# Differences of cumulated decays in a Mamba-2 block: rows broadcast from DRAM and GpSimd subtractions in place of float32r products

## The chip, the cores and the metric

The kernel runs on one core of a Trainium2 chip. The metric is the device time of one execution in microseconds (us); the time before is 1030.11 us, the median of 3 runs (1029.46 to 1030.83). The engines are PE (TensorE, matrix products; PEld its weight loads), DVE (VectorE), ACT (ScalarE), POOL (GpSimd) and SP (SyncE, which issues the weight loads). Each engine works through its own queue in order.

## The reference, cut to what matters

One layer: adaLN and RMSNorm on 256 context and 256 latent tokens, one input projection, a bidirectional Mamba-2 scan (32 heads in 8 groups of 4, chunks of 128 tokens) beside a gated MLP group, one output projection. The part that the change touches is the decay matrix of the diagonal blocks, in both directions (the backward one on flipped tokens):

```
a = dtc * A.reshape(G, R)
acs = jnp.cumsum(a, axis=2)
...
diff = acs_t[..., :, None] - acs_t[..., None, :]
mask = jnp.tril(jnp.ones((Q, Q), dtype=bool))
Lmat = jnp.exp(jnp.where(mask, diff, -jnp.inf))
y_diag = jnp.einsum('bcgqk,bcgrqk,bckgrp->bcqgrp', CB, Lmat, xdt)
```

Forward and backward differences have opposite signs on the two sides of the diagonal, so the kernel takes exp of the smaller of the two and applies the triangles to CB.

## The kernel before, in words

All large products run in three float32r passes (weights split into a high part on ACT, line 79, and a low part on DVE, line 80; lines 123 to 125 or 840 to 842 multiply). In this text a *main product* is one of these: 128 columns of weights against 512 columns. Weights come as 1 MB pieces from SP, each good for 48 main products of a full tile.

The program has four parts: the startup (scale and shift columns of adaLN, the token-rate column block `dt`, and seven tiles of the x/B/C columns), the 25 other x/B/C tiles (lines 652 to 669), 64 pieces of weights for the latents' v, u and gate columns (from 474 us on), and the output projection. A group g of the scan owns four tiles: two of x, one of B, one of C.

Between the main products the program places pieces of other work. `later(dt, fn)` notes a piece with a due time, `pump` emits it when the running count of product time reaches it; the order that the engines then get is also arranged by a scheduler, which moves instructions within a queue. `plan_tile` sets the due times of a group: `conv_silu`, `ssd_x` (transposes `ptx` to `xk`), `ssd_w` (POOL scales `xk` to `xw` and `xl`), `ssd_b`, `ssd_e` (the decay matrix `E`), `ssd_cb` (`pcb`, masked on DVE to `cbf` and `cbb`), `ssd_states` (`psc`, `psl`, then `hs` over ACT, POOL and DVE), `ssd_y` for the two chunks c (POOL makes a first part of `M`, DVE adds the other and multiplies by `E`; `pso` from `hs`; three sums into `y` on POOL) and `ssd_yd` (`psy` from `M`). A name such as M(1,0) below is `M` of group 1, chunk 0. Groups 0 to 2 follow each other closely, since most of their tiles are left over from the startup; groups 3 to 7 come every 47.7 us.

The decay matrix before: `dt_rows` (line 483) puts four copies of the step decays (`ar`, on POOL, line 486) against triangles of ones, so that `psa` has the cumulated sums of all 32 heads four times on 128 partitions; ACT and DVE split them into float32r parts and build two operands, `Lb` (minus the sums, and ones) and `Rm` (the sums of each of four heads beside ones, line 498, with a constant half from line 505). `ssd_e` (line 545) masks `Lb` to the heads of the group on ACT (`L`), then makes four products of 128x512 (`pd`, line 553), which give q minus k for four heads; ACT copies the backward one to `E`, DVE takes the minimum with the forward one (line 556), ACT takes exp.

```
q = spt([P, 4, P], f"pd{g}{c}{d}")
nc.tensor.matmul(q, lhsT=L[:, d * 2 + c, :], rhs=Rm[:, d * 2 + c], start=True, stop=True)
...
nc.scalar.copy(E[:, c], pd[1])
nc.vector.tensor_tensor(E[:, c], pd[0], E[:, c], op=ALU.min)
```

The functions that the change touches, with the line numbers of the profile:

Of the kernel before, what the change touches and what calls it, by code (L numbers as in the profile page):

```python
# [39 lines left out]
def tile_hybrid_ssd_mlp(  # L40
# [396 lines left out]
    dl4 = cpool.tile([P, 4], F32, name="dl4")
    gm = cpool.tile([P, NGRP], F32, name="gm")
    nc.vector.tensor_reduce(dl4, ident.rearrange("p (m h) -> p h m", h=4), axis=mybir.AxisListType.X, op=ALU.add)
    nc.vector.tensor_reduce(gm, ident.rearrange("p (b g h) -> p g b h", b=4, g=8), axis=mybir.AxisListType.XY, op=ALU.add)  # L440
# [13 lines left out]
    ar = y[:, 1, 256:512].rearrange("p (d r h) -> p d r h", d=2, r=4)  # L454
# [26 lines left out]
    # rows of acs, split exactly in two float32r parts, for the differences on the tensor engine:  # L481
    # rows (hi, lo) x 32 heads carry acs[q], rows (hi, lo) x 32 heads carry -acs[k]
    def dt_rows():
        psa = spt([P, 4, P], "psa")
        for c in range(2):
            nc.gpsimd.tensor_copy(ar, bc(at[:, 3 * c, :].rearrange("p (d h) -> p d h", d=2), 2, 4))
            for d in range(2):
                nc.tensor.matmul(psa[:, d * 2 + c, :], lhsT=ar[:, d].rearrange("p r h -> p (r h)"),
                                 rhs=tri_le if d == 0 else tri_ge, start=True, stop=True)
        X = yseg(6).bitcast(F32R)  # L490
        XL = yseg(7).bitcast(F32R)
        psf = psa.rearrange("p a b -> p (a b)")
        nc.scalar.copy(X, psf)
        nc.vector.tensor_tensor(XL, psf, yseg(6), op=ALU.subtract)
        for r0 in (32, 96):
            nc.vector.tensor_copy(X[r0 : r0 + 32], yseg(7)[r0 : r0 + 32])
        Xv = yseg(6).rearrange("p (a b) -> p a b", a=4)
        nc.vector.tensor_tensor(Rm[0:64], bc(Xv[0:64], 2, 4),
                                dl4[0:64].unsqueeze(1).unsqueeze(3).to_broadcast([64, 4, 4, P]), op=ALU.mult)
# [45 lines left out]
    def ssd_e(g):  # L545
        L = cv1.tile([P, 4, P], F32R, tag="L", name=f"L{g}")
        nc.scalar.mul(L, Lb, gm[:, g : g + 1])
        E = cv1.tile([P, 2, 4, P], F32, tag="E", name=f"E{g}")
# [473 lines left out]
```

## Time and profile before

| what | value |
|---|---|
| median of 3 runs | 1030.11 us (1029.46 to 1030.83) |
| span of the profiled execution, first to last instruction | 1026.3 us |
| median less span | 3.8 us |
| PE busy | 1000.6 us (97%) |
| DVE, ACT, POOL busy | 624.9, 474.9, 130.0 us |
| mean granted TensorE clock | 0.991 of full speed |

No time of its own is listed for the profiled execution beside its span; the 3.8 us by which the median of the runs exceeds the span are taken for what lies around the span. Busy time of PE is modelled from pipelined products that overlap, so a PE that is 97% busy can still be made faster by taking products away. What one product costs in the queue is read from the distance of the starts of its neighbours.

### The profile page before, as it was taken

Reading aid. Unit: us, or ns where it says so; the run is one execution under the profiler, and the core shown is the slowest. Engines: PE = TensorE matmul, PEld = TensorE weight load, DVE = VectorE, ACT = ScalarE, POOL = GpSimd, SP = SyncE. Lnnn points to the kernel's source line nnn. Section 1 sums busy time; section 2 is a strip of 40 time slices with the busy share of each in tenths; the row PEclk is TensorE's granted clock in tenths of the full one; section 3 lists DMA queues with packets and bytes.
Section 4 is the critical chain, followed back from the end, with each engine's and each line's share of the span. In section 5 each row is a group of like instructions: output and inputs, shape, how many; then the busy total and the mean of one; then the engine's idle time right before and its main releaser. Section 6 shows DMA issues by size and latency. Waiting matters only on the chain. (4 is left out here: it accounts for less than half of the span.)

```text
span 1026.3 us, 12875 instructions
## 1 busy us (share of the span) xinstructions
PE 1000.6 (97%) x5040; PEld 794.0 (77%) x5040; DVE 624.9 (61%) x927; ACT 474.9 (46%) x664; POOL 130.0 (13%) x169
## 2 busy tenths in 40 slices
PE   7999999999999999999999999999999999999995
PEld 2566777777888888787888888887888888888884
DVE  4443459997666565756566867666555564444446
ACT  4333346654534353435555344454565563444333
POOL 1000012272213233233000000000000000000004
PEclk9899999999999999999999999999999999999998
DMA  9999752221322222323878778774555545555542
GB/s 354 417 406 339 278 205 83 83 83 44 121 82 83 83 82 82 123 82 125 291 283 321 283 253 296 272 296 164 169 201 174 195 164 205 202 179 193 193 176 82
DMA packets 30028, 198.74 MB, mean 194 GB/s; under 512 B 3552, under 2 KB 3696, under 8 KB 7312
## 3 DMA queue, kind: packets, MB, share of 16 engines
q1 hardware_dynamic: 28224, 192.44, 50.8%
q0 software_dynamic: 1024, 4.28, 1.5%
q10 hardware_dynamic: 720, 1.20, 0.3%
q8 instruction: 39, 0.64, 0.2%
q14 instruction: 21, 0.17, 0.0%
HBM read 195.81 MB, written 2.10 MB: 193 GB/s over the span
## 5 line engine op out<-in xcount | busy, mean ns | idle before, releaser
L80 DVE TENSOR_TENSOR lo_w<-w,hi_w 128x1024 fp32r<-128x1024 f32 x242 | 298.6, 1240 | 222.4 <-ACT hi_w L79 222.1
L79 ACT CAST hi_w<-w 128x1024 fp32r<-128x1024 f32 x242 | 254.3, 1052 | 337.1 <-PE pa L842 143.8
L840 PE MATMUL pa<-hi_w,hhi 128*128 128x512 f32 x512 | 201.9, 395 | 0.0
L841 PE MATMUL pa<-lo_w,hhi 128*128 128x512 f32 x512 | 199.6, 390 | 0.0
L842 PE MATMUL pa<-hi_w,hlo 128*128 128x512 f32 x512 | 199.4, 389 | 0.0
L123 PE MATMUL psx<-hhi,hi_w 128*128 128x512 f32 (+1 forms) x400 | 152.5, 381 | 0.4 <-DVE acc L424 0.3
L124 PE MATMUL psx<-hlo,hi_w 128*128 128x512 f32 (+1 forms) x400 | 146.7, 367 | 0.0
L125 PE MATMUL psx<-hhi,lo_w 128*128 128x512 f32 (+1 forms) x400 | 146.3, 366 | 0.0
L840 PEld LDWEIGHTS pa<-hi_w,hhi 128*128 128x128 f32 x512 | 96.1, 188 | 20.9 <-issue 1.6
L842 PEld LDWEIGHTS pa<-hi_w,hlo 128*128 128x128 f32 x512 | 96.1, 188 | 20.2
L841 PEld LDWEIGHTS pa<-lo_w,hhi 128*128 128x128 f32 x512 | 96.2, 188 | 19.2 <-issue 0.2
L123 PEld LDWEIGHTS psx<-hhi,hi_w 128*128 128x128 f32 x400 | 75.6, 189 | 14.1 <-issue 2.4
L124 PEld LDWEIGHTS psx<-hlo,hi_w 128*128 128x128 f32 x400 | 75.6, 189 | 13.1 <-issue 2.2
L125 PEld LDWEIGHTS psx<-hhi,lo_w 128*128 128x128 f32 x400 | 75.5, 189 | 12.5 <-issue 0.2
L424 DVE SCALAR_TENSOR_TENSOR acc<-psx,pc,acc 128x248 f32<-128x248 f32 (+1 forms) x204 | 84.1, 469 | 0.8 <-ACT acc L411 0.2
L701 DVE SCALAR_TENSOR_TENSOR junk<-gate,cb 128x2048 bf16<-128x2048 f32 x16 | 36.7, 2292 | 28.4 <-DMA gate<-in_wada_dram 28.4
L912 POOL TENSOR_TENSOR og<-ob,G 128x512 f32<-128x512 f32 x7 | 10.5, 1535 | 333.1 <-DVE ob L907 333.1
L887 PE MATMUL pq<-hi_w,yal 128*128 128x512 f32 x128 | 50.7, 396 | 0.0
L885 PE MATMUL pq<-hi_w,yah 128*128 128x512 f32 x128 | 50.7, 396 | 0.0
L886 PE MATMUL pq<-lo_w,yah 128*128 128x512 f32 x128 | 50.7, 396 | 0.0
L278 DVE SCALAR_TENSOR_TENSOR xT<-xT,ha,y 128x256 f32<-128x256 f32 x32 | 14.1, 482 | 60.1 <-ACT ha L210 60.0
L885 PE MATMUL pm<-hi_w,hhi 128*128 128x512 f32 x128 | 50.0, 390 | 0.0
(221 smaller groups left out, 1305.6 us busy)
## 6 DMA issues: line engine op xcount, KB each, us to landing
w<-in_wlat_dram SPq DMA_DIRECT2D x64, 1024.0 KB, 4.8
ada<-in_wada_dram SPq DMA_DIRECT2D x32, 1024.0 KB, 7.8
w<-in_wout_dram SPq DMA_DIRECT2D x32, 1024.0 KB, 4.8
w<-in_wxbc_dram SPq DMA_DIRECT2D x25, 1024.0 KB, 4.8
gate<-in_wada_dram SPq DMA_DIRECT2D x16, 1024.0 KB, 6.0
wst<-in_wst_dram SPq DMA_DIRECT2D x16, 480.0 KB, 8.4
xT<-in_xch_dram SPq DMA_DIRECT2D x4, 1024.0 KB, 10.1
xf<-in_xtok_dram SPq DMA_DIRECT2D x2, 1024.0 KB, 4.7
```

The lines of the kernel that those rows point to most:

```text
L79: nc.scalar.copy(hi, raw)
L80: nc.vector.tensor_tensor(lo, raw, hi.bitcast(F32), op=ALU.subtract)
L123: nc.tensor.matmul(ps, lhsT=whi, rhs=hhi[k][:, s], start=start, stop=False)
L124: nc.tensor.matmul(ps, lhsT=whi, rhs=hlo[k][:, s], start=False, stop=False)
L125: nc.tensor.matmul(ps, lhsT=wlo, rhs=hhi[k][:, s], start=False, stop=stop)
L424: nc.vector.scalar_tensor_tensor(ao, zi, cw[:, k : k + 1], ao, op0=ALU.mult, op1=ALU.add)
L840: nc.tensor.matmul(pa[tk], lhsT=hhi[k][:, t], rhs=whi[:, w], start=k == 0, stop=False)
L841: nc.tensor.matmul(pa[tk], lhsT=hhi[k][:, t], rhs=wlo[:, w], start=False, stop=False)
L842: nc.tensor.matmul(pa[tk], lhsT=hlo[k][:, t], rhs=whi[:, w], start=False, stop=k == KT - 1)
L885: nc.tensor.matmul(p, lhsT=yh[:, t], rhs=whi[:, w], start=j == 0, stop=False)
L886: nc.tensor.matmul(p, lhsT=yh[:, t], rhs=wlo[:, w], start=False, stop=False)
L887: nc.tensor.matmul(p, lhsT=yl[:, t], rhs=whi[:, w], start=False, stop=j == 15)
```

## The change

`ssd_e` no longer uses PE. `dt_rows` forms the cumulated sums once, 32 heads on 32 partitions (`arow`), and GpSimd's queue writes them to a DRAM tile `acs` (64 KB). For each group `row_load` reads the group's four heads (8 KB) back onto all 128 partitions (`R`, 1 MB in SBUF, one buffer, again from GpSimd's queue). The new `dt_cols` turns `arow` by four small transposes into columns `acol`, k on partitions. In `ssd_e` POOL subtracts the columns from `R` in place (two instructions of 128x1024, one for each chunk) and DVE takes the minimum of the two directions from SBUF. The masked operand, the operands' construction, the copies from `pd` and their PSUM banks go. `row_load(0)` is called behind the write, `row_load(g + 1)` at the end of `ssd_states(g)`; `dt_rows` comes at 5 of the running count and `dt_cols` at 7, where `rm_const` and `dt_rows` stood. The rest of the diff takes comments away.

```diff
+    drp = ctx.enter_context(mkpool(name="drp", bufs=1, space=bass.MemoryType.DRAM))
...
-    Rm = cv1.tile([P, 4, 4, P], F32R, name="Rm")
-    Lb = cv1.tile([P, 4, P], F32, name="Lb")
...
+    acol = cv1.tile([P, 4, 32], F32, name="acol")
+    arow = cv1.tile([32, 4, P], F32, name="arow")
+    acs = drp.tile([32, 4 * P], F32, name="acs")
...
     def dt_rows():
-        psa = spt([P, 4, P], "psa")
-        for c in range(2):
-            nc.gpsimd.tensor_copy(ar, bc(at[:, 3 * c, :].rearrange("p (d h) -> p d h", d=2), 2, 4))
...
+        psa = spt([32, 4, P], "psa")
+        for d in range(2):
+            for c in range(2):
+                nc.tensor.matmul(psa[:, d * 2 + c, :], lhsT=at[:, 3 * c, d * 32 : (d + 1) * 32],
                                  rhs=tri_le if d == 0 else tri_ge, start=True, stop=True)
-        X = yseg(6).bitcast(F32R)
...
-        nc.vector.tensor_scalar(Lb[64:128], Xv[64:128], -1.0, None, op0=ALU.mult)
...
+        nc.scalar.copy(arow, psa)
+        nc.gpsimd.dma_start(acs, arow.rearrange("h a q -> h (a q)"))
+        row_load(0)
+
+    def dt_cols():
+        pst = spt([P, 4, 32], "pst")
+        for a in range(4):
+            nc.tensor.transpose(pst[:, a, :], arow[:, a, :], ident[0:32, 0:32])
+        nc.vector.tensor_copy(acol, pst)
...
+    def row_load(g):
+        R = cv1.tile([P, 4, 2, 2, P], F32, tag="R", name=f"R{g}")
+        nc.gpsimd.dma_start(R.rearrange("p h d c q -> p (h d c q)"),
+                            acs[4 * g : 4 * g + 4, :].rearrange("h x -> (h x)").unsqueeze(0).partition_broadcast(P))
+        rows_[g] = R
...
     def ssd_e(g):
-        L = cv1.tile([P, 4, P], F32R, tag="L", name=f"L{g}")
-        nc.scalar.mul(L, Lb, gm[:, g : g + 1])
+        R = rows_.pop(g)
         E = cv1.tile([P, 2, 4, P], F32, tag="E", name=f"E{g}")
         for c in range(2):
-            pd = []
-            for d in range(2):
-                q = spt([P, 4, P], f"pd{g}{c}{d}")
-                nc.tensor.matmul(q, lhsT=L[:, d * 2 + c, :], rhs=Rm[:, d * 2 + c], start=True, stop=True)
-                pd.append(q)
-            nc.scalar.copy(E[:, c], pd[1])
-            nc.vector.tensor_tensor(E[:, c], pd[0], E[:, c], op=ALU.min)
+            Rc = R[:, :, :, c, :]
+            col = acol.rearrange("p (d c) h -> p c h d", c=2)[:, c, 4 * g : 4 * g + 4, :]
+            nc.gpsimd.tensor_tensor(Rc, Rc, bc(col, 3, P), op=ALU.subtract)
+            nc.vector.tensor_tensor(E[:, c], Rc[:, :, 0, :], Rc[:, :, 1, :], op=ALU.min)
         nc.scalar.activation(E, E, AF.Exp)
...
         S["hs"] = hs
+        if g + 1 < NGRP:
+            row_load(g + 1)
...
-    later(5, rm_const)
+    later(5, dt_rows)
     later(6, dt_decay)
-    later(7, dt_rows)
+    later(7, dt_cols)
```

Where instructions stand in the queues, at three places. On PE, behind the main products of the tile in which the step decays become ready (`psd` are the products for the other decays, `ptx00` the first transposes of group 0), before:

```order
L475 MATMUL psd_1348<-y_127,ones_70 128x64
L488 MATMUL psa_1364<-tri_le_72,y_127 128x128
L488 MATMUL psa_1364<-tri_ge_75,y_127 128x128
L123 MATMUL psx8_1413<-hhi5_97,hi_w2_1290 128x512
L124 MATMUL psx8_1413<-hlo5_113,hi_w2_1290 128x512
L488 MATMUL psa_1364<-tri_le_72,y_127 128x128
L488 MATMUL psa_1364<-tri_ge_75,y_127 128x128
L125 MATMUL psx8_1413<-hhi5_97,lo_w2_1291 128x512
L521 MATMUL ptx00_1449<-ident_65,xbc0_1387 128x128 x4
```

and with the change:

```order
L484 MATMUL psa_1333<-tri_le_72,y_127 32x128 x2
L484 MATMUL psa_1333<-tri_ge_75,y_127 32x128 x2
L472 MATMUL psd_1354<-y_127,tri_lt_78 128x96
...
L472 MATMUL psd_1354<-y_127,ones_70 128x64
L123 MATMUL psx8_1412<-hhi5_97,hi_w2_1292 128x512
L124 MATMUL psx8_1412<-hlo5_113,hi_w2_1292 128x512
L493 MATMUL pst_1370<-ident_65,arow_1299 128x32 x4
L125 MATMUL psx8_1412<-hhi5_97,lo_w2_1293 128x512
L518 MATMUL ptx00_1448<-ident_65,xbc0_1386 128x128 x4
```

The four `psa` products stand together ahead of `psd`, and the new transposes `pst` stand where the second pair of `psa` stood.

On POOL, from the start of group 0 to its second `M`, before:

```order
L486 COPY y_127<-y_127 128x256 x2
L530 TENSOR_TENSOR xw0_1505<-xk0_1448,ed_1295 128x256 x4
L533 TENSOR_TENSOR xl0_1510<-xk0_1448,ed_1295 128x256 x2
L609 TENSOR_TENSOR y_127<-xk0_1448,dsk_84 128x256 x2
L575 TENSOR_TENSOR hs0_1652<-hs0_1652,ed_1295 128x256 x2
L597 TENSOR_TENSOR M00_1671<-cbb0_1637,dtt_1294 128x512
L610 TENSOR_TENSOR y_127<-y_127,yo00_1680 128x256
L597 TENSOR_TENSOR M01_1734<-cbb0_1637,dtt_1294 128x512
```

and with the change:

```order
L487 DMA acs_1300<-arow_1299 32x512
L500 DMA R0_1340<-acs_1300 128x2048
L527 TENSOR_TENSOR xw0_1504<-xk0_1447,ed_1297 128x256 x4
L530 TENSOR_TENSOR xl0_1509<-xk0_1447,ed_1297 128x256 x2
L604 TENSOR_TENSOR y_127<-xk0_1447,dsk_84 128x256
L548 TENSOR_TENSOR R0_1340<-R0_1340,acol_1298 128x8x128 x2
L604 TENSOR_TENSOR y_127<-xk0_1447,dsk_84 128x256
L500 DMA R1_1648<-acs_1300 128x2048
L568 TENSOR_TENSOR hs0_1641<-hs0_1641,ed_1297 128x256 x2
L548 TENSOR_TENSOR R1_1648<-R1_1648,acol_1298 128x8x128 x2
L592 TENSOR_TENSOR M00_1662<-cbb0_1626,dtt_1296 128x512
L592 TENSOR_TENSOR M01_1725<-cbb0_1626,dtt_1296 128x512
```

The subtractions of group 0, the read for group 1 and the subtractions of group 1 all stand ahead of M(0,0).

On POOL again, around the two `M` of group 1, before:

```order
L575 TENSOR_TENSOR hs1_1895<-hs1_1895,ed_1295 128x256 x2
L597 TENSOR_TENSOR M10_1938<-cbb1_1880,dtt_1294 128x512
L610 TENSOR_TENSOR y_127<-y_127,yo10_1947 128x256
L611 TENSOR_TENSOR y_127<-y_127,yo10_1947 128x256
L597 TENSOR_TENSOR M11_2006<-cbb1_1880,dtt_1294 128x512
```

and with the change:

```order
L500 DMA R2_1883<-acs_1300 128x2048
L527 TENSOR_TENSOR xw2_1802<-xk2_1763,ed_1297 128x256 x4
L530 TENSOR_TENSOR xl2_1807<-xk2_1763,ed_1297 128x256 x2
L568 TENSOR_TENSOR hs1_1876<-hs1_1876,ed_1297 128x256 x2
L548 TENSOR_TENSOR R2_1883<-R2_1883,acol_1298 128x8x128
L592 TENSOR_TENSOR M10_1921<-cbb1_1861,dtt_1296 128x512
L548 TENSOR_TENSOR R2_1883<-R2_1883,acol_1298 128x8x128
L605 TENSOR_TENSOR y_127<-y_127,yo10_1930 128x256
L606 TENSOR_TENSOR y_127<-y_127,yo10_1930 128x256
L592 TENSOR_TENSOR M11_1979<-cbb1_1861,dtt_1296 128x512
```

One subtraction for group 2 now precedes M(1,0) and the other stands between M(1,0) and M(1,1); likewise both subtractions for group 3 come between M(2,0) and M(2,1).

## Rows read from the trace of the kernel before

**Rows 1.** First lines of the page: span, then engine, busy us (share), instructions.

```profile
span 1026.3 us, 12875 instructions
PE 1000.6 (97%) x5040; PEld 794.0 (77%) x5040; DVE 624.9 (61%) x927; ACT 474.9 (46%) x664; POOL 130.0 (13%) x169
```

**Rows 2.** Windows: stretch, length, busy us (count) by engine, clock, DMA share, GB/s.

```profile
160.00:205.00 45.00, 43.51 (x213) 34.55 (x212) 42.44 (x93) 30.60 (x43) 11.86 (x17) 1.00 0.20 71
205.00:250.00 45.00, 44.39 (x230) 35.08 (x229) 39.42 (x75) 24.08 (x33) 27.94 (x34) 1.00 0.20 71
250.00:475.00 225.00, 224.95 (x1138) 185.35 (x1137) 141.44 (x257) 99.07 (x132) 58.80 (x73) 1.00 0.25 89
```

**Rows 3.** Waits of PE, 100 to 1000 us: us in total, times, longest.

```profile
PE pso L604 <- DVE hs L576: 1.9, 2, 1.4
PE psa L488 <- POOL y L486: 1.2, 1, 1.2
PE psx L123 <- DVE acc L424: 0.3, 1, 0.3
```

**Rows 4.** Timeline of PE: start us, us, instruction; four transposes, then the four `pd` of group 0.

```profile
180.08 0.60 PE L541 MATMUL ptb<-ident,xbc 128*128 128x128 f32 x4
180.44 1.17 PE L553 MATMUL pd<-Rm,L 128*128 128x512 f32 x4
181.45 0.39 PE L124 MATMUL psx<-hlo,hi_w 128*128 128x512 f32 x1
181.67 0.39 PE L125 MATMUL psx<-hhi,lo_w 128*128 128x512 f32 x1
```

**Rows 5.** Timeline of PE at the cumulated sums.

```profile
165.00 0.40 PE L124 MATMUL psx<-hlo,hi_w 128*128 128x512 f32 x1
166.58 0.49 PE L488 MATMUL psa<-tri_le,y 128*128 128x128 f32 x2 [1.19 <-POOL y L486]
```

**Rows 6.** Single lines of code: duration ns min/median/max, first and last start, forms.

```profile
L530 POOL TENSOR_TENSOR xw<-xk,ed x32: 608/615/662, 172.5 to 455.0; 128x256 f32<-128x256 f32 x32
L597 POOL TENSOR_TENSOR M<-cbb,dtt x16: 1037/1042/1887, 197.5 to 483.7; 128x512 f32<-128x512 f32 x16
L609 POOL TENSOR_TENSOR y<-xk,dsk x16: 610/838/1597, 176.0 to 458.3; 128x256 f32<-128x256 f32 x16
L80 DVE TENSOR_TENSOR lo_w<-w,hi_w x242: 1207/1226/1703, 146.9 to 1004.3; 128x1024 fp32r<-128x1024 f32 x121
```

**Rows 7.** DMA issues: count, KB each, median us from issue to landing.

```profile
cb<-in_crow_dram POOLq DMA_DIRECT2D x1, 1024.0 KB, 4.8
G<-in_gpost_dram POOLq DMA_DIRECT2D x1, 1024.0 KB, 6.8
out_dram<-xf SPq DMA_DIRECT2D x4, 256.0 KB, 2.3
dtc<-in_dtp_dram POOLq DMA_DIRECT2D x1, 32.0 KB, 7.1
```

**Rows 8.** Timeline of POOL: M(0,0), M(1,0), M(2,1), M(7,0).

```profile
197.47 1.04 POOL L597 TENSOR_TENSOR M<-cbb,dtt 128x512 f32<-128x512 f32 x1 [7.66 <-DVE cbb L589]
219.09 1.04 POOL L597 TENSOR_TENSOR M<-cbb,dtt 128x512 f32<-128x512 f32 x1
245.06 1.04 POOL L597 TENSOR_TENSOR M<-cbb,dtt 128x512 f32<-128x512 f32 x1 [2.79 <-PE psy L619]
473.17 1.89 POOL L597 TENSOR_TENSOR M<-cbb,dtt 128x512 f32<-128x512 f32 x1 [14.29 <-DVE cbb L589]
```

**Rows 9.** Timeline of PE: psy(0,0), psy(1,0) and psy(2,1), the products that take M.

```profile
201.87 1.00 PE L619 MATMUL psy<-xk,M 128*128 128x64 f32 x8
226.07 1.00 PE L619 MATMUL psy<-xk,M 128*128 128x64 f32 x8
249.40 1.00 PE L619 MATMUL psy<-xk,M 128*128 128x64 f32 x8
```

**Rows 10.** Timeline of DVE: M(1,0) is multiplied by E.

```profile
222.78 0.68 DVE L602 TENSOR_TENSOR M<-M,E 128x512 f32<-128x512 f32 x1
```

More of the change, by code (lines that the diff above doesn't have):

```diff
@@ L434, in tile_hybrid_ssd_mlp @@
     ed = cv1.tile([P, 384], F32, name="ed")
-    Rm = cv1.tile([P, 4, 4, P], F32R, name="Rm")
-    Lb = cv1.tile([P, 4, P], F32, name="Lb")
[L437 to L440, printed above, removed]
+    acol = cv1.tile([P, 4, 32], F32, name="acol")
+    arow = cv1.tile([32, 4, P], F32, name="arow")
+    acs = drp.tile([32, 4 * P], F32, name="acs")
     eu = ed.rearrange("p (u h) -> p u h", h=32)
@@ L453, in tile_hybrid_ssd_mlp @@
     eat = ed[:, 320:384].rearrange("p (d h) -> p d h", d=2)
-    ar = y[:, 1, 256:512].rearrange("p (d r h) -> p d r h", d=2, r=4)
     def dt_final():
@@ L483, in dt_rows @@
     def dt_rows():
-        psa = spt([P, 4, P], "psa")
-        for c in range(2):
-            nc.gpsimd.tensor_copy(ar, bc(at[:, 3 * c, :].rearrange("p (d h) -> p d h", d=2), 2, 4))
-            for d in range(2):
-                nc.tensor.matmul(psa[:, d * 2 + c, :], lhsT=ar[:, d].rearrange("p r h -> p (r h)"),
-                                 rhs=tri_le if d == 0 else tri_ge, start=True, stop=True)
-        X = yseg(6).bitcast(F32R)
[L491 to L499, printed above, removed]
-        nc.vector.tensor_scalar(Lb[64:128], Xv[64:128], -1.0, None, op0=ALU.mult)
-    nc.gpsimd.memset(Lb[0:64], 1.0)
-    def rm_const():
-        nc.gpsimd.tensor_copy(Rm[64:128], dl4[64:128].unsqueeze(1).unsqueeze(3).to_broadcast([64, 4, 4, P]))
+        psa = spt([32, 4, P], "psa")
+        for d in range(2):
+            for c in range(2):
+                nc.tensor.matmul(psa[:, d * 2 + c, :], lhsT=at[:, 3 * c, d * 32 : (d + 1) * 32],
+                                 rhs=tri_le if d == 0 else tri_ge, start=True, stop=True)
+        nc.scalar.copy(arow, psa)
[6 more added lines that the diff above has]
+        nc.vector.tensor_copy(acol, pst)
+    rows_ = {}
+    def row_load(g):
[3 more added lines that the diff above has]
+        rows_[g] = R
     gs_ = {}
@@ L545, in ssd_e @@
     def ssd_e(g):
-        L = cv1.tile([P, 4, P], F32R, tag="L", name=f"L{g}")
-        nc.scalar.mul(L, Lb, gm[:, g : g + 1])
+        R = rows_.pop(g)
         E = cv1.tile([P, 2, 4, P], F32, tag="E", name=f"E{g}")
         for c in range(2):
-            pd = []
-            for d in range(2):
-                q = spt([P, 4, P], f"pd{g}{c}{d}")
-                nc.tensor.matmul(q, lhsT=L[:, d * 2 + c, :], rhs=Rm[:, d * 2 + c], start=True, stop=True)
-                pd.append(q)
-            nc.scalar.copy(E[:, c], pd[1])
-            nc.vector.tensor_tensor(E[:, c], pd[0], E[:, c], op=ALU.min)
+            Rc = R[:, :, :, c, :]
+            col = acol.rearrange("p (d c) h -> p c h d", c=2)[:, c, 4 * g : 4 * g + 4, :]
+            nc.gpsimd.tensor_tensor(Rc, Rc, bc(col, 3, P), op=ALU.subtract)
+            nc.vector.tensor_tensor(E[:, c], Rc[:, :, 0, :], Rc[:, :, 1, :], op=ALU.min)
         nc.scalar.activation(E, E, AF.Exp)
```

## The prediction, made before the changed kernel was run

> **What bounds the kernel now.** I read the page first: the span is 1026.3 us, and PE is busy for 97% of it [rows 1]. [...] Third, the waits of PE: after the startup only three kinds are left, 3.4 us in all [rows 3]. So PE sets the end nearly everywhere. The exception to look at is 160 to 250 us, where groups 0 to 2 crowd together: DVE is busy for 42.4 of 45 us and then 39.4, and POOL goes from 11.9 to 27.9 us of 45 [rows 2]. The change adds its work to POOL, so this stretch decides what is left of the gain.
>
> **The change part by part.** The timed runs have a median 3.8 us above the profiled span; I take that as fixed and count against 1026.3.
>
> *The products that go.* Four `pd` per group start at 180.44 us and the next main product at 181.45; main products follow each other at 0.22 to 0.23 us [rows 4]. Four at that distance are 0.9 us; 1.01 holds the refill that any such block has. For 8 groups: 7.2 us (bounds 7.0 and 8.1). All of it is on PE's path.
>
> *The cumulated sums.* The second pair of `psa` starts at 166.58 us, behind a main product that began at 165.00; 0.23 us of that is the product, so PE stood for 1.35 us, for POOL's copy `ar` [rows 3, 5]. This copy is gone. In its place PE waits for ACT's `arow` before `pst`. Between the end of `psa` and `pst` lie now six `psd` products and two main products, some 1.7 us, and ACT needs about 0.6 for the copy: no wait expected. Four 128x128 transposes take 0.36 us (180.08 to 180.44) [rows 4]; the smaller `pst` is put at that. Net 1.0 us gained; if `arow` is late, up to 1.35 is lost again.
>
> *Two other waits.* The main product that waited 0.3 us for DVE's convolution [rows 3] had a DVE that was also building `Rm` and `Lb`; four instructions, about 4 us, go there, so 0.3 is gained. `pso` waited 1.9 us in two places for `hs`, the longest 1.4 in group 7 [rows 3]. There M(7,0) started on POOL at 473.17 after waiting for `cbb`, took 1.89 us beside DVE's splits, and `hs` of group 7 queued behind it [rows 8]. With the change the order puts `pcb` of group 7 five main products earlier and `pso` two later, so the chain has 1.6 us more room: 1.4 gained, and 0.5 in group 1 from the smaller `pd` load. Together 2.2 us (bounds 0.5 and 2.2).
>
> So far 7.2 + 1.0 + 2.2 = 10.4 us.
>
> *What POOL, DMA and DVE get instead.* No row shows a 128x1024 subtraction on POOL. Two-input instructions take 0.615 us for 256 elements per partition and 1.04 for 512 [rows 6], a slope that gives 1.9 us for 1024. That is the value without DVE's interference; L609 goes from 0.61 to 1.60 us for the same shape, and DVE's split from 1.21 to 1.70 [rows 6], when both work from SBUF. Bounds: 1.9 and 3.8 (twice). I take 1.9, with 0.5 more per group where the queue orders put DVE's splits and `M` beside it. A 1 MB load over POOL's queue lands after 4.8 or 6.8 us [rows 7]: 5.8. The write of 64 KB is bounded by 2.3 us (a store from SP) and 7.1 (a small load over POOL's queue at the start) [rows 7]; I take 3, since the 7.1 stood beside the startup's loads.
>
> Group 0: `psa` is done at about 164, `arow` at 164.8, the write at 168, R0 lands at 174.3, while POOL is at `xw` until 175.6. Subtractions to 179.5, minimum to 181.1, R1 requested then and landed at 187.4, its subtractions to about 192. M(0,0) started at 197.47 after 7.66 us of waiting for `cbb` [rows 8]: the subtractions of group 1 fit into that hole, and `cbb` comes some 3.3 us earlier since DVE has less to do. PE wants psy(0,0), before at 201.87 [rows 9], six main products sooner in the order (1.4) and 2.2 us sooner for the gains so far: 198.3; M needs 4.2 us on POOL and DVE from 194.2: ready at 198.4. Wait 0.1 to 0.2.
>
> Group 1: psy(0,0) and the transposes behind it let ACT finish `xk` of group 1 at about 202.5. POOL then has ten instructions of 0.61 us (`xw`, `xl`, `y`) and two sums of about 0.75 ahead of the request for R2: 202.5 + 6.1 + 1.5 + 0.5 = 210.6; R2 lands at 216.5. Eight more of 0.61 (`xw` and `xl` of group 2, `hs` of group 1) end at 215.5; the first subtraction waits for R2 and runs to 218.9, then M(1,0), before at 219.09 [rows 8]. It needed 4.4 us until DVE had it multiplied at 223.46 [rows 10]; 0.4 more beside the second subtraction: 223.7. PE, ahead by 1.0 + 0.3 + 0.5 + 3 x 0.9 less the waits so far, 3.7 us, wants psy(1,0), before at 226.07 [rows 9], at 222.4. Wait 1.3.
>
> Group 2: M(1,1) starts at 225.4, behind psy(1,0) and the two sums; DVE needs some 6 us until it has multiplied it and taken the minimum of group 2. R3 is requested at 232, lands at 237.8, two subtractions and the two sums that follow end at 243.6, where M(2,1) starts, before at 245.06 [rows 8]. PE, 2 us ahead, wants psy(2,1), before at 249.40 [rows 9], 4.3 us behind M(2,1) and with no room, at 247.4; it is ready at 243.6 + 4.3 = 247.9. Wait 0.5. Four small waits of 0.3 on the same chains (psy(0,1), `pso` of groups 1 and 2, psy(1,1)): 1.2. Together 3.2 us; bounds 0 and, with every term at its upper bound, about 20 (below).
>
> From group 3 on, groups are 47.7 us apart and the order computes `E` one group ahead: read and subtractions stand at the head of POOL's round. POOL was busy for 58.8 of 225 us [rows 2], 12.5 in 47.7; with 4.3 more and a read of 5.8 it still stands idle for half of the time: hidden. If that cover were gone, `xw` and then `psc` would be late. The minimum is the same work for DVE; ACT loses two copies and the mask per group; the DMA share rises by 1 MB per group from 0.25: hidden.
>
> Sum: 10.4 - 3.2 = 7.2 us; 1030.1 - 7.2 = **1022.9 us**.
>
> [...]
>
> **The rivals.**
>
> *Everything fits* (chance 0.17): the early waits vanish, because reads land in 4.8 us and PE's slack is larger than I read. For it: PE's own waits were tiny. 1030.1 - 10.4 = 1019.7.
>
> *The early groups eat the gain* (0.11): waits of 8.4 to 12.4 us there. It decides if both the subtractions cost 3 us or more and reads land at 6.8. Time 1030.1 to within 0.2%.
>
> *POOL becomes the pace of groups 0 to 2* (0.10), slower. The mechanism: POOL stops at each first subtraction until its read has landed, and `M`, `hs` and `xw` stand behind it. With the write at 7.1, reads at 6.8 and subtractions at 3.8: R0 lands at 179.7, subtracted at 187.3; R1 at 195.9, subtracted at 203.5; psy(0,0) at 207.8, a wait of 9.5. At psy(1,0) the wait is 2.4 + 0.8 longer: 4.5. At psy(2,1) 4.3 longer: 4.8. With 1.2 small ones 20. It is slower from 12.4 on; between that and 20, at 16: 1030.1 - 10.4 + 16 = 1035.7. For it: DVE at 94% there and L609's 1.60 us; against it: POOL's hole of 7.66 us.
> [...]
>
> *It does nothing on PE*: excluded as far as `pd` goes, since PE's order no longer holds them.
>
> **How the numbers follow.** The forecast, early waits of 0.5 to 8.4 us, has 0.62, its own range 1020 to 1028. A measurement tells 0.2% (2.1 us) from no change. Faster by more than that: 0.62 + 0.17 = 0.79; within: 0.11; slower: 0.10. The range for 8 in 10 takes in the first two rivals and leaves out the slower one and the fast edge: 1019.0 to 1031.5.
>
> **What would show it.** `pd` gone and no wait of PE for POOL at `psa`; the subtractions at 1.9 to 2.5 us; 1 MB reads at 5 to 7 us; PE's waits from 195 to 250 us some 3 us, on DVE's M or `hs`; none from 250 on, `pso` of group 7 included. I am wrong if subtractions take over 3 us, if `pst` waits for `arow`, or if PE waits in groups 3 to 7.

## The result and the profile after

The changed kernel takes **1033.82 us** (median of 5 runs, 1033.55 to 1035.46) against 1030.11 (1029.27 to 1030.83) for the kernel before beside it: a ratio of 1.004 with a 95% interval of 1.0028 to 1.0052. It is slower by 3.7 us; 1022.9 was forecast. The profiled span is 1031.9 us, where it was 1026.3 [rows 1]. Every listed run takes 1.6 to 1.8 us more than its span, not the 3.8 us put down ahead of the prediction. So the trace before is of an execution of some 1028.0 us (an estimate: 1026.3 + 1.7), 2.1 us under the median, and the two traces differ by 5.6 us where the medians differ by 3.7.

The windows of the changed kernel (stretch, length, busy us and count by engine, granted clock, DMA share, GB/s) answer to [rows 2]; under them are three windows of 5 us.

```profile
160.00:205.00 45.00, 40.60 (x191) 31.60 (x191) 39.61 (x84) 27.22 (x37) 21.65 (x19) 0.97 0.32 113
205.00:250.00 45.00, 40.29 (x193) 31.28 (x192) 31.62 (x58) 17.70 (x24) 32.31 (x38) 0.92 0.27 100
250.00:475.00 225.00, 222.72 (x1136) 183.62 (x1135) 151.64 (x272) 93.43 (x117) 84.23 (x90) 1.00 0.31 113
...
200.00:205.00 5.00, 2.71 (x11) 2.53 (x12) 5.00 (x11) 0.00 (x0) 0.66 (x1) 0.71 0.45 151
205.00:210.00 5.00, 5.00 (x19) 4.13 (x18) 5.00 (x11) 0.93 (x2) 2.07 (x4) 0.61 0.14 59
225.00:230.00 5.00, 4.79 (x12) 3.35 (x13) 1.95 (x3) 0.56 (x2) 3.61 (x3) 0.66 0.13 54
```

PE did less in 160 to 250 us than before (80.9 us against 87.9), and the granted clock, 1.00 before, is 0.97 and 0.92. The small windows show where: from about 202 and from about 226 us on PE was granted half its clock for a while (0.50 in each microsecond from 203 to 208 and from 226 to 229). The shares missing in the three, (0.29 + 0.39 + 0.34) x 5, are 5.1 us of a full clock, or some 10 us at half clock. What PE did ahead of both is in its waits and in its timeline (start us, us, instruction, idle before and what ended it); they answer to [rows 3, 9].

```profile
PE psy L614 <- DVE M L597: 4.8, 3, 3.4
PE pso L599 <- DVE hs L569: 2.7, 2, 2.2
PE pcb L579 <- ACT xbc L428: 2.6, 2, 1.6
PE ptx L518 <- ACT xbc L428: 1.4, 1, 1.4
PE psx L123 <- DVE acc L425: 0.4, 1, 0.4
```

```profile
202.29 1.97 PE L614 MATMUL psy<-xk,M 128*128 128x64 f32 x8 [3.37 <-DVE M L597]
225.21 1.38 PE L599 MATMUL pso<-hs,xbc 128*128 128x512 f32 x2 [2.20 <-DVE hs L569]
233.46 1.08 PE L614 MATMUL psy<-xk,M 128*128 128x64 f32 x8 [0.54 <-DVE M L597]
261.05 1.11 PE L614 MATMUL psy<-xk,M 128*128 128x64 f32 x8 [0.92 <-DVE M L597]
```

Waits rose from 3.4 to 11.9 us. PE stood 3.4 us at psy(0,0), where 0.1 to 0.2 was forecast, and 2.2 at pso(1,0); the clock fell behind each. psy(0,0) came 0.4 us later than before, psy(1,0) 7.4 and psy(2,1) 11.7. `pso` of group 7, which stood 1.4 us before, stood 0.5.

Now GpSimd and VectorE. The subtractions (first the single line: ns min/median/max), GpSimd's timeline, where M(0,0), M(1,0) and M(2,1) answer to [rows 8], and VectorE's timeline beside them:

```profile
L548 POOL TENSOR_TENSOR R<-R,acol x16: 1907/1911/5361, 175.4 to 409.5; 128x1024 f32<-128x1024 f32 x16
```

```profile
175.38 4.14 POOL L548 TENSOR_TENSOR R<-R,acol 128x1024 f32<-128x1024 f32 x2
...
191.10 7.23 POOL L548 TENSOR_TENSOR R<-R,acol 128x1024 f32<-128x1024 f32 x2 [3.33 <-DMA R<-acs]
198.29 1.04 POOL L592 TENSOR_TENSOR M<-cbb,dtt 128x512 f32<-128x512 f32 x1
...
228.26 1.04 POOL L592 TENSOR_TENSOR M<-cbb,dtt 128x512 f32<-128x512 f32 x1
229.26 1.92 POOL L548 TENSOR_TENSOR R<-R,acol 128x1024 f32<-128x1024 f32 x1
...
247.36 3.92 POOL L548 TENSOR_TENSOR R<-R,acol 128x1024 f32<-128x1024 f32 x2 [0.42 <-DMA R<-acs]
254.87 1.03 POOL L592 TENSOR_TENSOR M<-cbb,dtt 128x512 f32<-128x512 f32 x1
```

```profile
176.23 1.52 DVE L425 SCALAR_TENSOR_TENSOR acc<-y,pc,acc 128x252 f32<-128x252 f32 x1
177.66 0.47 DVE L425 SCALAR_TENSOR_TENSOR acc<-psx,pc,acc 128x252 f32<-128x252 f32 x1
178.05 1.74 DVE L425 SCALAR_TENSOR_TENSOR acc<-y,pc,acc 128x252 f32<-128x252 f32 x1
179.72 0.47 DVE L425 SCALAR_TENSOR_TENSOR acc<-psx,pc,acc 128x252 f32<-128x252 f32 x1
180.11 0.47 DVE L425 SCALAR_TENSOR_TENSOR acc<-y,pc,acc 128x248 f32<-128x248 f32 x1
...
186.65 6.90 DVE L425 SCALAR_TENSOR_TENSOR acc<-y,pc,acc 128x248 f32<-128x248 f32 x16
193.47 1.21 DVE L80 TENSOR_TENSOR lo_w<-w,hi_w 128x1024 fp32r<-128x1024 f32 x1
194.60 0.41 DVE L583 TENSOR_TENSOR cbf<-pcb,tri_le 128x256 f32<-128x256 f32 x1
...
229.34 2.77 DVE L595 SCALAR_TENSOR_TENSOR M<-cbf,dtt,M 128x128 f32<-128x128 f32 x4 [3.05 <-POOL M L592]
...
246.97 4.46 DVE L595 SCALAR_TENSOR_TENSOR M<-cbf,dtt,M 128x128 f32<-128x128 f32 x4 [0.70 <-POOL M L592]
```

Read the first five rows of VectorE. Three convolution steps take a tile that lies in SBUF (`y`), two take PSUM (`psx`). Beside the subtractions of group 0 (175.4 to 179.5 us) the PSUM ones keep their 0.47 us and the SBUF ones need 1.52 and 1.74; behind them an SBUF one needs 0.47 again. The four products of M, cbf and M both in SBUF, take 2.77 and 4.46 us beside subtractions; the same four take 1.14 at 199.36 us, where GpSimd has nothing. It holds the other way too: the pair of group 1 started at 191.10 beside convolutions from `y` and took 7.23 us, not 3.8. Its first subtraction took 5.36 us (the maximum of the single line), not 1.91: VectorE went on with six convolution steps from `y`, at their 0.47 us, and its split at 193.47, all with both inputs in SBUF, and the subtraction ended 1.8 us behind the split, while VectorE's next instruction (`cbf`) read PSUM. So GpSimd waited for seven instructions, not for one.

To place the loss I count TensorE's main products, 3840 in every trace with those of 256 columns. Start of five of them in us, and the difference to the kernel before in brackets (column "fills" is experiment e5, below):

| main product | before | after | fills |
|---|---|---|---|
| 499th | 195.41 | 193.44 (-2.0) | 193.36 (-2.0) |
| 703rd | 259.86 | 271.62 (+11.8) | 261.60 (+1.7) |
| 1451st | 446.08 | 453.66 (+7.6) | 443.64 (-2.4) |
| 1633rd | 492.65 | 498.44 (+5.8) | 488.48 (-4.2) |
| last | 1013.99 | 1019.40 (+5.4) | 1009.41 (-4.6) |

All of the loss lies between 193 and 272 us: 13.7 us in groups 0 to 2. From the 703rd to the 1451st product four groups give back 4.2 us, 1.05 each, and group 7, up to the 1633rd, another 1.8.

### The profile page after: what moved, and what is told of

Same layout as the page of the kernel before. It is cut to its first block, busy times and chain, and to the rows that moved or that the text cites. A ratio compares the mean times of both kernels' runs of the same rounds, so it can differ in the third digit from the quotient of the medians.

```text
span 1031.9 us, 12829 instructions
## 1 busy us (share of the span) xinstructions
PE 998.5 (97%) x5012; PEld 791.4 (77%) x5012; DVE 629.0 (61%) x921; ACT 463.3 (45%) x640; POOL 167.5 (16%) x190
## 2 busy tenths in 40 slices
DMA packets 31212, 207.19 MB, mean 201 GB/s; under 512 B 3696, under 2 KB 3840, under 8 KB 7472
## 3 DMA queue, kind: packets, MB, share of 16 engines
HBM read 204.20 MB, written 2.16 MB: 200 GB/s over the span
## 5 line engine op out<-in xcount | busy, mean ns | idle before, releaser
L125 PE MATMUL psx<-hhi,lo_w 128*128 128x512 f32 (+1 forms) x400 | 148.4, 371 | 0.0
L123 PEld LDWEIGHTS psx<-hhi,hi_w 128*128 128x128 f32 x400 | 76.5, 191 | 13.7 <-issue 2.7
L881 PE MATMUL pm<-lo_w,hhi 128*128 128x512 f32 x128 | 50.0, 390 | 0.0
```

The source lines that it names most:

```text
L123: nc.tensor.matmul(ps, lhsT=whi, rhs=hhi[k][:, s], start=start, stop=False)
L125: nc.tensor.matmul(ps, lhsT=wlo, rhs=hhi[k][:, s], start=False, stop=stop)
L881: nc.tensor.matmul(p, lhsT=yh[:, t], rhs=wlo[:, w], start=False, stop=False)
```

## The experiments

The theory: GpSimd's subtractions and VectorE hold each other off SBUF where groups 0 to 2 crowd, TensorE stands for it, and its clock falls behind the stall. The rivals: the order on GpSimd, GpSimd's own time, the reads.

**e1, order.** The subtractions of group 1 behind M(0,0) on GpSimd (M's instruction is kept in `mi`):

```diff
-            nc.gpsimd.tensor_tensor(Rc, Rc, bc(col, 3, P), op=ALU.subtract)
+            with tc.issue_after(mi[g - 1, 0].ins) if g == 1 else ExitStack():
+                nc.gpsimd.tensor_tensor(Rc, Rc, bc(col, 3, P), op=ALU.subtract)
```

> The changed kernel with one order on GpSimd altered: the two subtractions of group 1 are issued behind M(0,0) instead of ahead of it. Nothing else moves by hand. Theory (queue and clock): in the changed kernel M(0,0) stands behind the subtractions of group 1, which took 7.2 us there; TensorE stands 3.4 us for it at psy(0,0) and then loses another 3.4 us at half clock. So: no stall over 0.5 us at psy(0,0), no 1.2 GHz stretch behind it, 1033.8 - 6.8 = 1027 us (1026 to 1029, if the later stalls stay). Rival (reads): what stops GpSimd is the landing of the 1 MB reads; the order is worth under 1 us: 1033 to 1034. Rival (VectorE): the convolutions and M are late on VectorE for the shared access to SBUF, wherever the subtractions stand: the stall moves to psy(0,1) or pso(1,0), gain at most 2: 1032.

Measured: 1034.67 us, ratio to before 1.0042 (1.0023 to 1.0062). My theory fell in this form. GpSimd's and VectorE's timelines:

```profile
196.11 1.04 POOL L593 TENSOR_TENSOR M<-cbb,dtt 128x512 f32<-128x512 f32 x1 [7.65 <-DVE cbb L585]
197.11 3.83 POOL L549 TENSOR_TENSOR R<-R,acol 128x1024 f32<-128x1024 f32 x2
```

```profile
197.18 4.43 DVE L596 SCALAR_TENSOR_TENSOR M<-cbf,dtt,M 128x128 f32<-128x128 f32 x4 [0.49 <-POOL M L593]
```

M(0,0) did start 2.2 us earlier, and the pair shrank from 7.23 to 3.83. But VectorE's four products of M now stood beside it and took 4.43 us instead of 1.14; TensorE stood 3.8 us at the same psy(0,0). The order alone moved the collision.

**e2, filling the stall.**

```diff
+        if (g, c) == (0, 0):
+            for _ in range(10):
+                nc.tensor.matmul(psy, lhsT=ones, rhs=ones[:, 0:1].to_broadcast([P, 256]), start=True, stop=True)
```

> The changed kernel with ten idle products (ones by ones, 256 columns, into psy's own bank ahead of its real products) placed on TensorE just before psy(0,0), so that it works through most of the 3.4 us in which it stood. They compute nothing that is used. Theory (clock): the stretch of 6.8 us at 1.2 GHz behind psy(0,0) follows from the stall; filled, it stays at 2.4 GHz and 3.4 us come back: 1030.4 us (1029.5 to 1031.5). Rival: the lower clock there has another cause than the stall: it is there again, 1033.8, or up to 2 us slower where the filling outlasts the stall.

Measured: 1042.75 us, 1.0123 (1.0096 to 1.015). TensorE's timeline:

```profile
198.82 4.51 PE L615 MATMUL psy<-ones 128*128 128x256 f32 x20
203.18 1.00 PE L617 MATMUL psy<-xk,M 128*128 128x64 f32 x8
213.09 1.97 PE L617 MATMUL psy<-xk,M 128*128 128x64 f32 x8 [4.24 <-DVE M L597]
```

psy(0,0) then took 1.00 us and not 1.97: with no stall ahead of it the granted clock stayed at 1.00 (200 to 210 us). But the filling lasted 4.5 us, 1.1 longer than the stall, the scheduler moved M(0,1) behind the sums of `y` on GpSimd, and TensorE stood 4.2 us at psy(0,1) and lost the clock there (0.73 from 210 to 215 us, 0.59 from 215 to 220). So the clock fell behind the stall here too; what it costs by itself this run does not tell.

**e3, folding.** No subtraction on GpSimd (`sgap` is c1 - c0, `nac` is -c1):

```diff
-            nc.gpsimd.tensor_tensor(Rc, Rc, bc(col, 3, P), op=ALU.subtract)
-            nc.vector.tensor_tensor(E[:, c], Rc[:, :, 0, :], Rc[:, :, 1, :], op=ALU.min)
-        nc.scalar.activation(E, E, AF.Exp)
+            for h in range(4):
+                j = 4 * g + h
+                nc.vector.scalar_tensor_tensor(E[:, c, h, :], R[:, h, 0, c, :], sgap[:, c, j : j + 1], R[:, h, 1, c, :],
+                                               op0=ALU.add, op1=ALU.min)
+                nc.scalar.activation(E[:, c, h, :], E[:, c, h, :], AF.Exp, bias=nac[:, c, j : j + 1])
```

> The changed kernel without any subtraction on GpSimd: the minimum becomes min(r0 + (c1 - c0), r1) by eight VectorE instructions of 128 columns in place of two of 512, and c1 is subtracted in the exponential, as the bias of eight ScalarE instructions of 128 columns in place of one of 1024. Reads of the rows stay. Theory (queue): GpSimd's queue is that of the kernel before again; psy(0,0) has no stall over 0.5 us, no stretch at 1.2 GHz, 1022 to 1026 us. Rival (reads): the landing of the rows now stops VectorE instead, 1030 or more. Rival (VectorE): it was VectorE's time that ran out in groups 0 to 2; 1.1 us more per group there gives back what the free access to SBUF brings: 1028 to 1033.

Measured: 1022.7 us, 0.9934 (0.9912 to 0.9957): 11.1 us less than the changed kernel, with the same reads through DRAM. Both rivals are out as the cause of the loss. psy(0,0) waited 0.28 us. One stall is left, and it is VectorE's: a convolution stood behind the eight minima of group 1, which took 5.34 us:

```profile
PE psx L123 <- DVE acc L425: 3.1, 1, 3.1
```

**e4, hybrid.** Products for groups 0 to 2, rows and subtractions from group 3:

```diff
     def ssd_e(g):
+        if g >= 3:
+            return ssd_er(g)
```

> Groups 0 to 2 by the float32r products of the kernel before, groups 3 to 7 by rows through DRAM and GpSimd's subtraction; the tile of rows takes the place of the products' right side after group 2. Theory: the loss lies in groups 0 to 2 alone, and from group 3 on each group gains the 1.05 us that main products show, group 7 0.8 more: 1030.1 - 5 x 1.05 - 0.8 = 1024 us (1023 to 1025.5). Rival (a loss of the whole, for instance from the reads beside the weights): 1028 or more.

Measured: 1027.64 us, 0.998 (0.9968 to 0.9993); 3.6 us short. Against the kernel before it stood +0.2 us at the 619th main product and +5.0 at the 631st, then gained as expected. (The trace is of an execution of 1031.68 us, 4.0 over the median; it loses 4.5 us between 578 and 822 us, far behind the groups.) Between these two places the subtractions of group 3 split the two products of `hs` of group 2 on GpSimd, and TensorE waited for the second:

```profile
240.33 1.12 PE L641 MATMUL pso<-hs,xbc 128*128 128x512 f32 x2 [2.43 <-DVE hs L609]
```

**e5, fills.** Each subtraction replaced by two fills, so that the differences are not computed; the queues of TensorE, VectorE and ScalarE keep their order:

```diff
-            nc.gpsimd.tensor_tensor(Rc, Rc, bc(col, 3, P), op=ALU.subtract)
+            nc.gpsimd.memset(Rc, 0.0)
+            nc.gpsimd.memset(Rc[:, 0:3], 0.0)
```

> The changed kernel with each subtraction of 1024 columns replaced by two plain fills of the same tile, of 1024 and 768 columns: the difference of the cumulated decays is not computed, the exponential gets zeros. The orders of TensorE, VectorE and ScalarE are those of the changed kernel, and so is GpSimd's, with fills where subtractions stood. From the fills of the profile (0.21 us for 128 columns, 0.54 for 512) a pair of fills should take some 1.8 us, about the 1.91 of a subtraction, behind the same reads, but it reads nothing from SBUF. Theory (shared access): VectorE's instructions with both inputs in SBUF are no longer held; the four products of M beside it take 1.14 us again (not 2.8 to 4.5), the convolutions of the held tiles 0.4 each; a pair takes 3.6 and not 7.2 us in group 1; psy(0,0) has no stall over 1 us; 1023 to 1027 us. Rival (GpSimd's own time, or the reads): the queue is as long as before: 1031 to 1034.

Measured: 1023.17 us, 0.994 (0.9924 to 0.9955). Two windows, then GpSimd's fills, VectorE's products of M(1,0) beside fills, and pso(1,0) on TensorE:

```profile
160.00:205.00 45.00, 44.72 (x223) 35.52 (x222) 41.87 (x96) 29.49 (x40) 22.83 (x28) 1.00 0.33 119
205.00:250.00 45.00, 41.43 (x201) 32.34 (x200) 33.71 (x67) 19.56 (x25) 33.55 (x42) 0.92 0.31 117
```

```profile
189.14 1.85 POOL L547 MEMSET R<- 128x1024 f32 x2 [1.13 <-DMA R<-acs]
190.93 1.42 POOL L548 MEMSET R<- 128x768 f32 x2
194.88 1.04 POOL L592 TENSOR_TENSOR M<-cbb,dtt 128x512 f32<-128x512 f32 x1 [2.53 <-DVE cbb L584]
...
222.75 0.74 POOL L548 MEMSET R<- 128x768 f32 x1
223.42 0.95 POOL L547 MEMSET R<- 128x1024 f32 x1
```

```profile
222.84 1.14 DVE L595 SCALAR_TENSOR_TENSOR M<-cbf,dtt,M 128x128 f32<-128x128 f32 x4 [2.07 <-POOL M L592]
```

```profile
219.69 1.22 PE L599 MATMUL pso<-hs,xbc 128*128 128x512 f32 x1 [2.21 <-DVE hs L569]
```

GpSimd was busy for no less time in these windows (22.8 and 33.6 us against 21.7 and 32.3 in the changed kernel, with more of TensorE's work in them), behind the same reads, and the kernel is 10.7 us faster. The work for group 1 took 3.3 us, M(0,0) waited for VectorE and not for GpSimd's queue, and M(1,0)'s products took 1.14 us beside fills, not 2.77. So most of the loss comes neither from GpSimd's own time nor from the reads, but from reading SBUF beside VectorE: 9.9 of the 13.7 us in the table go with it.

The other 3.8 us stay. TensorE waited 1.4 us for a convolution and 2.2 at pso(1,0), as in the changed kernel, and the granted clock fell behind that (0.92 in the window of 205 to 250 us; main products started 0.43 us apart from 221.99 to 224.55 us, and 0.23 from 226.14 to 227.07). pso(1,0) starts at 219.69 us here and at 219.65 in the kernel before; GpSimd's part of the `hs` that it waits for starts at 218.00 and 217.95. That chain became no earlier, and TensorE's lead is given up there. GpSimd's queue has no gap ahead of it, from 203.3 us on here and from 202.2 before; that the queue alone keeps the chain there is not shown (e12 speaks against it).

**e6, folding, minimum of group 1 later.**

```diff
-            later(d0 + 2, lambda: ssd_e(g))
+            later(d0 + (5 if g == 1 else 2), lambda: ssd_e(g))
```

> The folded kernel (no subtraction on GpSimd) with the exponent of group 1 due 3 units of the planner later, so that VectorE convolves xBC tile 10 ahead of the eight minima of group 1 instead of behind them. In the folded kernel these minima took 5.3 us beside GpSimd and the convolution behind them kept TensorE 3.1 us from the next tile, after which it was granted half clock for 3.4 us. Theory: both go, 3.1 + 1.7 = 4.8 us less whatever comes late next: 1018 to 1020 us. Rival: the minima are then late for M(1,0), and TensorE stands at psy(1,0) for what it gained: 1021.5 to 1024.

Measured: 1022.07 us, 0.993 (0.9915 to 0.9946). The convolution's stall and the low clock went (1.00 in both windows), but TensorE stood 1.77 us at pso(1,0) and 1.40 at psy(1,0): the rival's case.

**e7, hybrid, subtractions of group 3 behind M(2,1)**, by the same lines as e1 with `mi[2, 1]`.

> The hybrid (products for groups 0 to 2, rows from group 3 on) with the two subtractions of group 3 issued behind M(2,1). In the hybrid they stood between the two products of hs of group 2 on GpSimd; TensorE waited 2.4 us for hs and was granted half clock for 3.4 us after it. Theory: with the subtractions where nobody waits, that wait and the half clock go: 4.1 us less, 1022.5 to 1024. Rival: the slow place has another cause (the transposes for the columns, the tile of rows waiting for the products): 1027.

Measured: 1027.77 us, 0.9982 (0.9969 to 0.9995). The wait for `hs` went (0.5 us at most is left) and another came. GpSimd's and VectorE's timelines:

```profile
245.91 1.92 POOL L537 TENSOR_TENSOR R<-R,acol 128x1024 f32<-128x1024 f32 x1
247.79 0.79 POOL L648 TENSOR_TENSOR y<-y,yo 128x256 f32<-128x256 f32 x1
248.54 1.96 POOL L537 TENSOR_TENSOR R<-R,acol 128x1024 f32<-128x1024 f32 x1
250.47 0.76 POOL L649 TENSOR_TENSOR y<-y,yo 128x256 f32<-128x256 f32 x1
```

```profile
245.99 5.39 DVE L638 SCALAR_TENSOR_TENSOR M<-cbf,dtt,M 128x128 f32<-128x128 f32 x4 [0.96 <-POOL M L635]
```

Four instructions of GpSimd, 5.43 us together, and four products of M in 5.39: as I read it the engines took turns here, one instruction each, so that a product of 0.3 us waited for a whole subtraction of 1.92 or 1.96. TensorE stood 2.9 us at psy(2,1).

**e8, pieces.**

```diff
-            nc.gpsimd.tensor_tensor(Rc, Rc, bc(col, 3, P), op=ALU.subtract)
+            for h in range(4):
+                nc.gpsimd.tensor_tensor(Rc[:, h], Rc[:, h], bc(col[:, h], 2, P), op=ALU.subtract)
```

> The changed kernel with each GpSimd subtraction of 1024 columns cut into four of 256; every order else is as it was. Theory (VectorE is held for a whole GpSimd instruction): a VectorE instruction with both inputs in SBUF waits for at most one piece, 0.6 us by the 256-column rows, and not 1.9; the four products of M beside them take 2 to 3.5 us and not 2.8 to 4.5, while GpSimd's own sum rises from 3.8 to some 5 us per group. On balance 1029 to 1033 us. Rival (VectorE is held by GpSimd's total work, in whatever pieces): the products of M take as long as before and GpSimd longer: 1034 to 1037.

Measured: 1033.92 us, 1.0042 (1.0028 to 1.0056). At the same two places as in the changed kernel, M's products took 2.56 and 2.56 us, not 2.77 and 4.46, as the theory has it. But GpSimd's own wait did not shrink with the pieces: the eight of group 1 took 10.1 us beside the convolutions, not 7.2, and one piece alone 6.06 us (ns min/median/max):

```profile
L549 POOL TENSOR_TENSOR R<-R,acol x64: 605/612/6063, 176.3 to 411.9; 128x256 f32<-128x256 f32 x64
```

It started at 189.15 us and was held, as in the changed kernel, until VectorE's run of convolution steps and its split was over at 194.7. From then on eight pieces need 4.6 us and two whole subtractions 3.8, so M(0,0) came 0.9 us later. The range was missed on the slow side.

**e9, subtraction on ScalarE**, with `acol` negated:

```diff
-            nc.gpsimd.tensor_tensor(Rc, Rc, bc(col, 3, P), op=ALU.subtract)
+            for h in range(4):
+                for d in range(2):
+                    j = 4 * g + h
+                    nc.scalar.activation(Rc[:, h, d], Rc[:, h, d], AF.Identity, bias=acol[:, 2 * d + c, j : j + 1])
```

> The changed kernel with the subtraction on ScalarE, sixteen instructions of 128 columns per group with the column as bias, in place of two on GpSimd; rows, reads, minimum on VectorE and exponential are those of the changed kernel. From rows of 0.32 us for such an instruction ScalarE gets some 5 us more per group. Theory (shared access of GpSimd and VectorE): with the subtraction on an engine that does not hold VectorE, the loss of groups 0 to 2 goes: 1021.5 to 1026 us. Rival (the detour through DRAM or the wait for the landing costs it): 1030 or more. Rival (ScalarE becomes late with hi_w, xk and the convolutions' start): stalls of TensorE behind ScalarE of 3 us and more, 1026 to 1030.

Measured: 1026.21 us, 0.9969 (0.996 to 0.9979). 7.6 us come back with GpSimd out of it. The rest is between theory and the rival of a late ScalarE: the instructions took 0.39 us each, not 0.32, and from 262 us on TensorE stood 2.2 us for ScalarE's `xbc`, where the changed kernel did not.

**e10, hybrid, subtractions behind the last sum of group 2.**

> The hybrid with the two subtractions of group 3 behind the last sum of group 2 on GpSimd, so that they stand beside no product of M of group 2. In the hybrid with them behind M(2,1) the four products of M(2,1) took 5.4 us and not 1.1, TensorE stood 2.9 us at psy(2,1) and was granted half clock for 3.4 us. Theory (shared access, and the clock behind the stall): both go, 2.9 + 1.7 = 4.6 us less: 1022.5 to 1024 us. Rival: the hybrid loses about 4 us for another reason, for instance in the first read or the transposes: 1026.5 to 1028.

Measured: 1027.95 us, 0.998 (0.9969 to 0.9991). A miss by the same turns: the sums do not wait for M's products, so sums and subtractions stood beside all four of them, which took 5.47 us.

**e11, hybrid, subtractions behind xw and xl of group 3.**

> The hybrid with the two subtractions of group 3 behind xw and xl of group 3 on GpSimd, some 25 us after the products of M(2,1). With them just behind the last sum of group 2 these four products still took 5.5 us, each held by one of two sums and two subtractions, and TensorE stood 3.0 us for them, with half clock for 3.4 us after it. Theory (shared access): no subtraction stands beside a product of M that TensorE waits for soon; both losses go, 1027.9 - 3.0 - 1.7 = 1023.2 us (1022.3 to 1024). Rival: the four us of the hybrid have another cause and come back at another place: 1026.5 to 1028.5.

Measured: 1034.9 us, 1.0056 (1.0036 to 1.0076). At its place the theory held: M(2,1)'s products took 2.16 us, psy(2,1) did not wait. But VectorE's queue now had the minimum of group 3 ahead of a convolution and stood for the subtraction; TensorE stood for the convolution, and 2.4 us more for `hs` of group 3. VectorE, then TensorE:

```profile
269.43 2.39 DVE L538 TENSOR_TENSOR E<-R 128x512 f32<-128x512 f32 x1 [7.12 <-POOL R L537]
```

```profile
276.63 0.70 PE L123 MATMUL psx<-hhi,hi_w 128*128 128x512 f32 x1 [4.79 <-DVE acc L425]
```

No run shows a hybrid without a collision or a wait; that it would give 1023 us stays an estimate.

**e12, folding as in e6, `hs` of group 1 earlier on GpSimd** (xw of group 2 due 6 units later).

> The folded kernel with the late minimum of group 1, and besides with xw of group 2 due 6 units of the planner later, so that GpSimd does hs of group 1 before the last two of the four xw of group 2 and before xl. There TensorE stood 1.8 us at pso(1,0) for hs and 1.4 us at psy(1,0) for M. Theory: GpSimd is 4 instructions of 0.6 us earlier with hs and the first wait goes: 1020 to 1021.5 us. Rival: what TensorE gains there it waits at psy(1,0), since M(1,0) hangs on GpSimd behind the same work: 1021.7 to 1022.5.

Measured: **1021.7 us**, 0.9929 (0.9913 to 0.9945). It is the fastest here, faster than both kernels; the intervals of e3, e6 and e12 overlap. But the wait at pso(1,0) stayed (1.75 us). GpSimd had its part of `hs` done at 214.7 us, 2.6 earlier than in e6; VectorE did its own only behind the minima of group 1:

```profile
214.94 3.36 DVE L552 SCALAR_TENSOR_TENSOR E<-R,sgap 128x128 f32<-128x128 f32 x8
...
218.89 0.74 DVE L573 TENSOR_TENSOR hs<-psl,hs 128x256 f32<-128x256 f32 x2
```

## Why the prediction was wrong

- *The products that go*: right. 0.9 us per group was forecast (7.0 to 8.1 for eight), 1.05 came from each of groups 3 to 6, a little over the upper bound. The refill "that any such block has", by which the 0.9 is less than the 1.01 read off, is shown in no view.
- *The cumulated sums*: right in kind; `psa` no longer waits for GpSimd and `pst` did not wait for `arow`. From the 331st to the 427th main product the lead grew by 0.6 us, not 1.0.
- *Two other waits*: group 7 gained 1.8 us in all, where 0.9 + 1.4 was forecast; 0.5 of its wait is left. The 0.5 us in group 1 did not come: pso(1,0) waited 2.2 us, in e5 too. Nor did the 0.3 us of the convolution; 0.4 was waited.
- *Prices of the new parts alone*: right for the subtraction, 1.91 us (1.9), and the read, 5.4 (5.8). The write took 1.9 (3), under its lower bound of 2.3.
- *Groups 3 to 7 hidden*: right. GpSimd rose from 58.8 to 84.2 us of 225, and from 262 us on TensorE waited 0.5 us. Its one larger wait there, 1.4 us for the first transposes of group 3, hangs on a convolution that was late from group 2.
- **The step that failed** is "I take 1.9, with 0.5 more per group where the queue orders put DVE's splits and `M` beside it". What the contention cost was read from rows in which GpSimd's instructions were short [rows 6], and it was priced as a half microsecond; but VectorE's instructions waited for whole ones of GpSimd (four products of M took 5.39 us beside four GpSimd instructions in e7, 1.14 alone), and a GpSimd subtraction of 1.91 us waited for a whole run of VectorE's (5.36). The trace before had it in small: four products of M took 2.16 us beside two sums of `y` (246.13 us) and 1.14 alone. The pair of group 1 took 7.23 us instead of 3.8, M's products 1.6 and 3.3 us more, and the convolutions from `y`, which I had not named, 1.1 and 1.3 more for a step. Through them M(0,0), forecast at 194.2, came at 198.3 and psy(0,0), forecast ready at 198.4, at 202.3. Early waits were put at 3.2 us; from 180 to 262 us they came to 11.4 (3.9 in e5, without the collision).
- *A term that was missing*: the clock. No line of the sum has it, and some 10 us behind the two stalls ran at half clock, 5.1 us of a full one. The views give the clock as a share of full speed (0.50 there); no run shows the GHz of the expectations of e1 to e3.
- That e5, without the collision, measured 1023.17 us against the 1022.9 of the forecast is in part luck: its early waits were 3.9 us where 3.2 was put, a stretch at half clock came on top, fills of 3.3 us stood for subtractions of 3.8, and the sum counts from a median 2.1 us above the execution it was read from.
- *The rivals*: "POOL becomes the pace of groups 0 to 2", 1035.7 us with a chance of 0.10, came nearest in time and place. But its working took slow reads (6.8 us; 5.4 in the median) and made GpSimd's time the pace, which e5 excludes for 9.9 of the 13.7 us. I had the rows that bore on it, L609's 0.61 to 1.60 us and the split's 1.21 to 1.70 [rows 6], and gave them to a bound and a rival instead of asking which VectorE rows stand beside each subtraction in the order.

## What to carry to other kernels

Moving elementwise work to an idle GpSimd was not free for VectorE here: list what VectorE has beside it, mark the instructions with both inputs in SBUF, and put one whole GpSimd instruction on each of them (an estimate from e7, where four products of M took 5.39 us beside four GpSimd instructions and not 1.14); count too that a GpSimd instruction that meets an unbroken run of them may wait for the whole run, as the one of 1.91 us that took 5.36 did. It was cheap where VectorE had slack (groups 3 to 7 here) and dear where VectorE's result was awaited; reordering only moved the collision (e1, e7, e10). Better to fold the work into instructions that exist already, as a scalar operand and a bias, or to give it to another engine (e3: 1022.7 us; e9: 1026.2). And ask what TensorE waits for next: where that chain becomes no earlier, as `hs` of group 1 here, the time that was freed is given up again.

## What I had not expected of the hardware

Where VectorE had to wait, the two seem to have taken turns: four products of M of 0.3 us ended with the fourth GpSimd instruction in e7 (5.39 and 5.43 us). GpSimd did not always get its turn: a subtraction of 1.91 us that met a run of VectorE's took 5.36, and a piece of 0.61 us took 6.06 (e8), while one that came between products of M at 247.36 us was hardly held (the pair took 3.92). What decides that is not shown. A GpSimd fill, which reads nothing from SBUF, did not hold VectorE (1.14 us for the products of M(1,0) beside fills in e5, 2.77 beside a subtraction). And the granted clock fell to 0.50 behind stalls of 3.37 and 2.20 us in the changed kernel, but not behind waits of 1.77 and 1.40 in e6 (1.00 in the window of 205 to 250 us). Where it changes isn't settled: behind waits of 1.36 and 0.92 us at 260 us the changed kernel kept its clock (1.00 in the window of 260 to 265) and e1 lost it (0.68).
